# A planned decoder kernel: TensorE's operations count as ready half a microsecond behind their operands, and the index heads' rotation tables are made first

## The chip, the cores and the metric

The kernel runs on one core of one Trainium2 chip. Of the core, five engines matter: TensorE (PE in the profile, with its weight loads as PEld), VectorE (DVE), ScalarE (ACT), GpSimd (POOL) and the queue that issues most of the DMAs (SP). The metric is the device time of one execution in microseconds (us), as the median of some runs. Lower is better.

## The reference

Two layers of a decoder trunk for one sequence of 256 tokens with 1024 channels, in float32. Each layer adds three things to the residual x: a token mixer, a cross-attention into 256 memory tokens, and a SwiGLU feed-forward network of width 2816.

```python
for i in range(2):
    h = rms_norm(x, norm_mix[i])
    x = x + (dsa_moba_mixer(h, ...) if i == 0 else nsa_mixer(h, ...))
    x = x + memory_cross_attention(rms_norm(x, norm_mem[i]), rms_norm(mem, norm_mem_src[i]), ...)
    x = x + swiglu(rms_norm(x, norm_ffn[i]), ffn_w_in[i], ffn_w_out[i])

def dsa_moba_mixer(h, ...):
    aq, ak, av, iq, ik, iw, bq, bk, bv = _split(h @ w_in, AB_SIZES)
    aq, ak = partial_rope(rms_norm(aq)), partial_rope(rms_norm(ak))     # 8 heads, one key head
    iq, ik = partial_rope(iq), partial_rope(ik)                         # index heads: 8 of 32
    o_a = dsa_attention(aq, ak, av, iq, ik, iw)                         # each query keeps 64 keys
    bq, bk = partial_rope(rms_norm(bq)), partial_rope(rms_norm(bk))
    o_b = moba_attention(bq, bk, bv)                                    # 8 heads, block-sparse
    return concat(o_a, o_b) @ w_out

def nsa_mixer(h, ...):                     # 16 heads in 4 groups: compressed, selected and window branch
    q, kc, vc, ks, vs, kw, vw, gt = _split(h @ w_in, C_SIZES)
    ...
    return (g0 * o_compressed + g1 * o_selected + g2 * o_window) @ w_out
```

The rotation (partial_rope) turns the first quarter of each head by angles from the positions. So it needs tables of sine and cosine; for the heads with a norm, the kernel multiplies the norm's gain into these tables, and the index heads have no norm.

## The kernel before

The 256 tokens are two tiles of 128 (t0, t1). Every float32 product is made of three matmuls on halves (mm3): each operand is split into a high part rounded to TensorE's format and the rest, and high by high, high by low and low by high are added up. The weights stream from memory through three raw buffers (raw, 512 KB each) and are split into six buffers (whl): the high part is a cast on ACT or DVE (move), the low part a subtract on DVE. The thread that does this is the pusher. One such unit holds two blocks of 128 rows by up to 512 columns, and it serves 12 matmuls, six for each token tile.

What each engine does, and in which order, is fixed before the program runs, by a planner in Python. Each part of the computation is a thread (a generator) with a rank; it yields operations (Op), waits for flags (has, done) and waits for buffers. Est keeps an estimated clock for each engine and the estimated end of each write and read of each buffer. Steps.run repeats one step: for each engine it takes, among the operations whose estimated start lies within 0.03 us of that engine's earliest, the one of lowest rank; of these it issues the one that starts first, on its engine, and lets that thread go on. Op.best gives the estimated start, from the engine's clock and from the operands (Est.after, Est.when). An operation with two ways (either, move, tt) goes to the engine on which it would end first, so a shift of the order also moves operations between ACT, DVE and POOL. The engines then work their lists in order and wait for each other by semaphores.

The accumulators are eight: two each of mm (matmuls with weights), sp (scores), tp (transposes) and po (attention products). Names that come up below: h are the normed tokens, place and t work buffers, x the residual, di the index heads' doubled queries on their way to a transpose, hss and mrk the sums of squares of the memory keys' heads and their inverse roots (a power on POOL), stack_T the transposes of split queries (t, with identr), keys_T and mem_k those of keys (place, with ident), kvT the index scores, bv the values of the block-sparse heads. ia and ib are the index heads' rotation tables, ra and rb those with gains.

The function tables makes all rotation tables. It computes the angles, then sine and cosine on ACT. Then it waits until both norms' halves of the first tile are done, multiplies gains (kv), spreads the gains over the partitions with one small matmul (own to growt, in a tp accumulator), copies ia and ib, makes ra and rb, and the masks cm, cmn, cmi with affine selects on POOL. Its flag "tables" is what the index heads' rotation waits for, in ev_small of mixer0 (the thread that takes the narrow columns: ak, av, iq, ik, iw). Mixer 0's other rotations come later in the program and find the tables made. In the profile all planned operations carry one line, L250, so they are told apart by their buffers.

## Time and profile before

| | before |
|---|---|
| median of three runs | 789.94 us (789.73 to 790.62) |
| the profiled execution | 790.53 us, of which the span is 788.8 us |
| PE busy | 759.2 us, 96% of the span |
| DVE busy | 536.8 us, 68% |
| ACT busy | 428.5 us, 54% |
| POOL busy | 120.8 us, 15% |

The stages follow each other: mixer 0 to about 119 us, the memory attention and feed-forward of layer 0 to about 373 us, mixer 1 from there to about 527 us with its attention from about 445 to 503 us, then memory attention and feed-forward of layer 1. A timeline row gives the start, the duration, the engine, the instruction with its buffers, how many such instructions stand in a row, and in brackets the engine's idle time before it with what ended it.

### The profile page before, as it was taken

The numbers are of one execution on the slowest core, as the hardware profiler recorded it, in microseconds if no ns is written. First come the engines' busy times: TensorE is split into PE (matmuls) and PEld (weight loads), VectorE is DVE, ScalarE is ACT, GpSimd is POOL, SyncE is SP. The second block draws the span as 40 slices with busy tenths as digits, with TensorE's granted clock in tenths as the row PEclk, the third lists the DMA queues.
The fourth block names the chain that finished last, engine by engine and source line by source line (L and its number), as shares of the span: only waits on it lengthen the run. The fifth ranks groups of instructions, "written<-read, shape, count | busy, mean of one in ns | idle before, by whom it ended". The sixth has DMA issues, their size and how long they took to land.

```text
span 788.8 us, 11748 instructions
## 1 busy us (share of the span) xinstructions
PE 759.2 (96%) x4227; PEld 627.7 (80%) x4227; DVE 536.8 (68%) x1117; ACT 428.5 (54%) x819; POOL 120.8 (15%) x163
## 2 busy tenths in 40 slices
PE   6999999999999999999999998999999999999998
PEld 5777778897888889787878777877888888889886
DVE  6899999768655554455728899868677556546542
ACT  5666895665544443343627599846556434435440
POOL 1545320110000000000016355201201000000000
PEclk9999999999999999999999999999999999999999
DMA  6734246526556544767416512035435565536651
GB/s 206 226 112 132 85 145 196 169 91 198 162 162 211 187 150 155 205 237 220 129 45 181 195 47 95 27 121 162 159 114 150 167 210 185 166 116 226 219 183 53
DMA packets 70634, 122.32 MB, mean 155 GB/s; under 512 B 8548, under 2 KB 15792, under 8 KB 70576
## 3 DMA queue, kind: packets, MB, share of 16 engines
q1 hardware_dynamic: 70544, 121.58, 49.1%
q8 instruction: 33, 0.54, 0.3%
q14 instruction: 25, 0.20, 0.1%
q0 software_dynamic: 32, 0.00, 0.0%
HBM read 120.51 MB, written 1.05 MB: 154 GB/s over the span
## 4 chain that ended last, share of the span: by engine, by line
PE 69%; DVE 13%; DMA 5%; ACT 4%; issue 3%; POOL 3%; SPq 1%; ACTq 0%; POOLq 0%; DVEq 0%
PE mm L250 54%; PE po L250 8%; PE tp L250 6%; DVE whl L250 5%; DVE place L250 5%; DMA raw<-in_ffn_w_out 3%; ACT place L250 2%; ACT whl L250 2%; PE sp L250 2%; DMA raw<-in_ffn_w_in 1%; DVE rc L250 1%; POOL rope L250 1%; POOL place L250 1%; DMA raw<-in_ab_w_in 1%; DVE x L250 1%
## 5 line engine op out<-in xcount | busy, mean ns | idle before, releaser
L250 PE MATMUL mm<-whl,h 128*128 128x512 f32 (+3 forms) x1776 | 401.2, 379 | 4.7 <-DVE whl L250 4.7
L250 DVE TENSOR_TENSOR whl<-raw,whl 128x1024 fp32r<-128x1024 f32 (+3 forms) x232 | 271.2, 1173 | 138.1 <-ACT whl L250 134.0
L250 PEld LDWEIGHTS mm<-whl,h 128*128 128x128 f32 x1776 | 311.2, 189 | 62.0 <-DVE whl L250 4.6
L250 ACT ACTIVATE whl<-raw 128x1024 fp32r<-128x1024 f32 (+3 forms) x204 | 206.2, 1013 | 161.6 <-PE mm L250 43.4
L250 PE MATMUL mm<-whl,place 128*128 128x512 f32 (+1 forms) x840 | 194.4, 374 | 2.1 <-DVE x L250 1.2
L250 PEld LDWEIGHTS mm<-whl,place 128*128 128x128 f32 x840 | 142.4, 188 | 29.6 <-DVE x L250 2.1
L250 ACT ACTIVATE place<-tp 128x512 f32<-128x512 f32 (+3 forms) x123 | 56.9, 492 | 60.7 <-PE tp L250 60.5
L250 PE MATMUL po<-whl,place 128*128 128x512 f32 x264 | 68.1, 395 | 0.0
L250 PEld LDWEIGHTS po<-whl,place 128*128 128x128 f32 x264 | 49.3, 188 | 11.3
L250 PE MATMUL tp<-ident,place 128*128 128x128 f32 x340 | 54.0, 277 | 3.6 <-DVE place L250 1.6
L250 POOL TENSOR_TENSOR rh<-vh,mhalf 128x1 f32<-128x1 f32 x12 | 10.4, 867 | 274.4 <-DVE vh L250 257.7
L250 PEld LDWEIGHTS tp<-ident,place 128*128 128x128 f32 x340 | 39.2, 141 | 15.0 <-issue 4.3
L250 ACT ACTIVATE place<-place,mx 128x128 f32<-128x128 f32 (+1 forms) x96 | 42.6, 448 | 3.9 <-DVE mx L250 3.6
L250 POOL TENSOR_TENSOR place<-place,rc 128x512 f32<-128x512 f32 (+2 forms) x31 | 27.3, 883 | 38.1 <-DVE rc L250 20.2
L250 DVE CAST whl<-raw 128x1024 fp32r<-128x1024 f32 (+2 forms) x28 | 20.1, 719 | 17.0 <-PE mm L250 13.3
L250 DVE CUSTOM_DVE_ANT_0 place<-sp,cm,rq 128x128 f32<-128x128 f32 (+1 forms) x80 | 30.2, 404 | 1.2 <-PE sp L250 1.2
L250 DVE TENSOR_TENSOR x<-mm,x 128x512 f32<-128x512 f32 x36 | 24.3, 684 | 9.6 <-PE mm L250 9.6
L250 ACT ACTIVATE place<-mm,rh 128x512 f32<-128x512 f32 (+1 forms) x26 | 17.0, 655 | 25.3 <-PE mm L250 25.3
L250 ACT ACTIVATE h<-place 128x512 fp32r<-128x512 f32 x22 | 13.8, 628 | 29.0 <-DVE place L250 28.9
L250 PE MATMUL sp<-place,place 128*128 128x256 f32 x160 | 27.2, 296 | 1.6 <-DVE mx L250 1.2
L250 DVE SCALAR_TENSOR_TENSOR place<-mm,rh,place 128x512 f32<-128x512 f32 (+1 forms) x24 | 16.9, 704 | 16.9 <-PE mm L250 16.9
L250 ACT ACTIVATE place<-mm 128x512 f32<-128x512 f32 (+2 forms) x46 | 23.8, 556 | 7.4 <-PE mm L250 7.2
(203 smaller groups left out, 607.7 us busy)
## 6 DMA issues: line engine op xcount, KB each, us to landing
raw<-in_ffn_w_in SPq DMA_DIRECT2D x80, 512.0 KB, 4.4
raw<-in_ffn_w_out SPq DMA_DIRECT2D x44, 512.0 KB, 4.4
raw<-in_ab_w_in SPq DMA_DIRECT2D x16, 512.0 KB, 3.7
raw<-in_mem_w_kv SPq DMA_DIRECT2D x16, 512.0 KB, 4.6
raw<-in_nsa_w_in SPq DMA_DIRECT2D x16, 512.0 KB, 4.0
raw<-in_ab_w_out SPq DMA_DIRECT2D x8, 512.0 KB, 3.8
raw<-in_mem_w_q SPq DMA_DIRECT2D x8, 512.0 KB, 4.1
raw<-in_mem_w_o SPq DMA_DIRECT2D x8, 512.0 KB, 4.0
```

The costliest lines, as they stand in the source:

```text
L250: return f(*a, **{q: v() if q in ("start", "stop") and callable(v) else v for q, v in k.items()})
```

## The change

Two things are changed. First, the planner's estimate of when an operation of PE could start (Op.best) counts each operand that another engine wrote, and each buffer that another engine still reads, as ready 0.5 us later than estimated. Only the choice is touched: when an operation is issued, its estimated end (Est.issue) is worked out as before. Second, tables is split. ia and ib are made right behind sine and cosine, without the gains and without the wait for the norms; a new flag, "angles", says so, and the index heads' rotation waits for this one. The rest becomes gains, a thread of its own of rank 3, with the wait for the norms and the old flag "tables", for which the rotations of ak, of the queries and of bk now wait. The thread tables has rank 2 instead of 3.

```diff
+SLACK = {"PE": 0.5}
...
     def best(self):
         if self.deps is None:
-            self.deps = [self.est.after(e, outs, ins) for e, outs, ins, _, _ in self.ways]
+            self.deps = [self.est.after(e, outs, ins, SLACK.get(e, 0.0)) for e, outs, ins, _, _ in self.ways]
...
-    def when(self, ap, tab, e="", raw=True):
+    def when(self, ap, tab, e="", raw=True, slack=0.0):
         k, lo, hi = self.span(ap)
-        return max([t + HOP.get(g + e, 0.0) * (raw or e != g) for a, b, t, g in tab.get(k, ())
+        return max([t + HOP.get(g + e, 0.0) * (raw or e != g) + slack * (e != g) for a, b, t, g in tab.get(k, ())
                     if a < hi and lo < b or raw and g == "PE" != e], default=0.0)
...
-    def after(self, e, outs, ins):
+    def after(self, e, outs, ins, slack=0.0):
         t = 0.0
         for a in ins:
-            t = max(t, self.when(a, self.wr, e))
+            t = max(t, self.when(a, self.wr, e, True, slack))
         for a in outs:
-            t = max(t, self.when(a, self.wr, e, False), self.when(a, self.rd, e, False))
+            t = max(t, self.when(a, self.wr, e, False, slack), self.when(a, self.rd, e, False, slack))
...
         yield from ready(AF.Exp)
-        yield has(("mix0", 0), 2)
         nsin = cp.tile([P, NT, HALF], F32, name="nsin")
         yield V.tensor_scalar(nsin, sin, -1.0, None, op0=OP.mult)
+        for h in range(2):
+            yield V.tensor_copy(ia[:, :, h, :], cos[:, :, ::2])
+            yield V.tensor_copy(ib[:, :, h, :], (sin if h else nsin)[:, :, ::2])
+        done("angles")
+        spawn(gains(sin, nsin, cos), 3)
+
+    def gains(sin, nsin, cos):
+        yield has(("mix0", 0), 2)
...
         gv = growt.rearrange("p j (a b) -> p j a b", a=2)
-        for h in range(2):
-            yield V.tensor_copy(ia[:, :, h, :], cos[:, :, ::2])
-            yield V.tensor_copy(ib[:, :, h, :], (sin if h else nsin)[:, :, ::2])
...
-            yield has("tables")
+            yield has("angles")
             yield from rope(c[:, 128:384].rearrange("p (h d) -> p h d", h=IH), IH, ia[:, t], ib[:, t], IHALF)
...
             yield V.tensor_scalar(k, k, rk, 8.0, op0=OP.mult, op1=OP.mult)
+            yield has("tables")
             yield from rope(k, 1, ra[:, t, 1], rb[:, t, 1], HALF)
...
+                yield has("tables")
                 yield from rope(q, 8, ra[:, t, 2 * j], rb[:, t, 2 * j], HALF)
...
+            yield has("tables")
             yield from rope(q, 8, ra[:, t, 3], rb[:, t, 3], HALF)
...
-    spawn(tables(), 3)
+    spawn(tables(), 2)
```

Both changes act on the order of all engines. Three places show how.

DVE in mixer 0, around the low parts of bv's weight units (whl, numbered by buffer). Before; the last row but five is bv's second unit, the last row the third unit:

```order
L250 TENSOR_TENSOR whl_701<-raw_521,whl_701 128x1024
L250 SCALAR_TENSOR_TENSOR kvT<-place_847,iw,kvT 128x256
L250 SCALAR_TENSOR_TENSOR place_774<-tp_850,kv,place_772 128x2x128
L250 SCALAR_TENSOR_TENSOR place_775<-tp_850,kv,place_773 128x2x128
L250 SCALAR_TENSOR_TENSOR kvT<-place_847,iw,kvT 128x256
L250 MATCH_REPLACE kvT<-m_834,kvT 128x128
L250 TENSOR_TENSOR whl_862<-raw_632,whl_862 128x1024
L250 MAX m_897<-kvT 128x8
L250 TENSOR_REDUCE hss<-place_889 128x8
L250 MATCH_REPLACE kvT<-m_897,kvT 128x128
L250 TENSOR_TENSOR t_884<-place_790,t_884 128x8x64
L250 TENSOR_TENSOR whl_904<-raw_699,whl_904 128x1024
```

Now; the first row is the first unit, the last but two the second:

```order
L252 TENSOR_TENSOR whl_702<-raw_594,whl_702 128x1024
L252 MAX m_728<-kvT 128x8
L252 TENSOR_REDUCE hss<-place_718 128x8
L252 SCALAR_TENSOR_TENSOR kvT<-place_723,iw,kvT 128x256
L252 TENSOR_TENSOR t_742<-place_621,rk_631 128x1024
L252 SCALAR_TENSOR_TENSOR kvT<-place_723,iw,kvT 128x256
L252 MATCH_REPLACE kvT<-m_728,kvT 128x128
L252 TENSOR_SCALAR he<-vh_294 128x1
L252 TENSOR_TENSOR whl_733<-raw_673,whl_733 128x1024
L252 SCALAR_TENSOR_TENSOR kvT<-place_767,iw,kvT 128x256
L252 SCALAR_TENSOR_TENSOR place_755<-tp_757,kv,place_753 128x2x128
```

The second unit's subtract stands in row 128 of the list instead of 153; the third's stands in row 158 in both (the last row of before's excerpt; now it is 30 rows further than the second's).

PE in the attention of layer 1, in the second half of its heads of t0 (sp scores, tp transposes, po products). Before:

```order
L250 MATMUL sp_5140<-place_4113,place_4946 128x256
L250 MATMUL sp_5140<-place_4109,place_4946 128x256
L250 MATMUL sp_5140<-place_4113,place_4946 128x256
L250 MATMUL tp_5114<-ident,place_4963 128x128
L250 MATMUL tp_5160<-ident,place_5021 128x128 x4
L250 MATMUL po_4641<-place_5115,vv 64x128 x4
L250 MATMUL po_4641<-place_5083,vv 64x128 x4
L250 MATMUL tp_5191<-ident,place_5052 120x128
L250 MATMUL tp_5206<-identr,t_5181 128x128 x4
L250 MATMUL tp_5223<-identr,t_5181 128x128 x4
```

Now, between transposes of the same heads:

```order
L252 MATMUL tp_5118<-ident,place_4993 128x128 x2
L252 MATMUL mm_5168<-whl_4467,place_4936 128x512 x2
L252 MATMUL mm_5168<-whl_4467,place_4937 128x512
L252 MATMUL mm_5168<-whl_4467,place_4936 128x512
L252 MATMUL tp_5184<-ident,place_5008 128x128 x4
L252 MATMUL mm_5168<-whl_4467,place_4936 128x512
L252 MATMUL po_4689<-place_5119,vv 64x128 x4
L252 MATMUL po_4689<-place_5094,vv 64x128 x4
L252 MATMUL tp_5203<-ident,place_5074 128x128 x4
L252 MATMUL mm_5168<-whl_4467,place_4937 128x512
L252 MATMUL tp_5237<-ident,place_5106 120x128
L252 MATMUL mm_5168<-whl_4485,place_4936 128x512 x2
```

Matmuls of the out projection (mm, from whl and place), which before began some 60 matmuls later, stand between transposes and products now.

PE at the memory keys of layer 1 (the product with weights into mm, then the transposes of the first key tile). Before:

```order
L250 MATMUL mm_5869<-whl_5750,h_113 128x512 x2
L250 MATMUL mm_5869<-whl_5750,h_114 128x512
L250 MATMUL tp_5872<-ident,place_5810 128x128 x4
L250 MATMUL mm_5869<-whl_5750,h_113 128x512 x2
L250 MATMUL mm_5869<-whl_5750,h_114 128x512
```

Now:

```order
L252 MATMUL mm_5869<-whl_5749,h_113 128x512 x2
L252 MATMUL mm_5869<-whl_5749,h_114 128x512
L252 MATMUL mm_5869<-whl_5749,h_113 128x512 x2
L252 MATMUL tp_5872<-ident,place_5814 128x128 x4
L252 MATMUL mm_5869<-whl_5749,h_114 128x512
L252 MATMUL mm_5869<-whl_5776,h_113 128x512 x2
```

The transposes come behind five matmuls instead of three. Those of the second key tile moved from behind 18 further matmuls to behind 20. DVE at the same place, before:

```order
L250 TENSOR_TENSOR whl_5858<-raw_5794,whl_5858 128x1024
L250 TENSOR_REDUCE hss<-place_5877 128x4
L250 SCALAR_TENSOR_TENSOR mkT_5760<-tp_5872,kv,mkT_5759 128x4x128
L250 TENSOR_SCALAR he<-vm_1291 128x1
L250 TENSOR_SCALAR hss<-hss,he 128x4
L250 TENSOR_TENSOR whl_5881<-raw_5845,whl_5881 128x1024
L250 TENSOR_TENSOR place_5870<-place_5870,mrk 128x512
```

Now:

```order
L252 TENSOR_TENSOR whl_5858<-raw_5785,whl_5858 128x1024
L252 TENSOR_REDUCE hss<-place_5877 128x4
L252 TENSOR_SCALAR he<-vm_1243 128x1
L252 CAST whl_5881<-raw_5845 128x1024
L252 SCALAR_TENSOR_TENSOR mkT_5755<-tp_5872,kv,mkT_5754 128x4x128
L252 TENSOR_SCALAR hss<-hss,he 128x4
L252 TENSOR_TENSOR whl_5881<-raw_5845,whl_5881 128x1024
L252 TENSOR_TENSOR place_5870<-place_5870,mrk 128x512
```

The cast of a weight unit (CAST), which was an operation of ACT, stands between the first tile's work and hss of the second.

## Rows read from the trace of the kernel before

**Rows 1.** The page, its first part: busy time, share of the span and instructions of each engine

```profile
PE 759.2 (96%) x4227; PEld 627.7 (80%) x4227; DVE 536.8 (68%) x1117; ACT 428.5 (54%) x819; POOL 120.8 (15%) x163
```

**Rows 2.** Windows of the span: length, busy time of each engine, granted clock, DMA share, GB/s

```profile
0.00:14.65 14.65, 7.38 (x24) 5.96 (x25) 7.32 (x25) 6.48 (x11) 2.44 (x11) 1.00 0.68 206
28.00:107.00 79.00, 74.19 (x430) 58.93 (x430) 76.91 (x258) 61.20 (x144) 39.63 (x58) 0.98 0.44 131
72.70:76.10 3.40, 3.39 (x14) 2.77 (x14) 3.40 (x11) 2.37 (x6) 1.08 (x1) 0.50 0.64 190
200.00:220.00 20.00, 20.00 (x93) 16.38 (x92) 12.02 (x15) 8.16 (x12) 0.00 (x0) 1.00 0.62 189
429.00:503.00 74.00, 68.74 (x552) 58.06 (x552) 67.62 (x247) 58.75 (x183) 32.12 (x39) 1.00 0.32 108
450.00:491.00 41.00, 37.98 (x338) 32.21 (x336) 39.72 (x174) 35.54 (x124) 24.95 (x30) 1.00 0.26 87
```

**Rows 3.** Waits of PE: who waits for whom, us in total, times, longest us

```profile
PE mm L250 <- DVE whl L250: 4.9, 5, 1.9
...
PE tp L250 <- DVE place L250: 2.8, 4, 1.2
```

**Rows 4.** Timeline of PE, 26 to 41 us: start, us, instruction, count, idle before it

```profile
27.55 0.45 PE L250 MATMUL tp<-place,one 76*128 76x112 f32 x2 [1.24 <-DVE place L250]
...
27.76 7.34 PE L250 MATMUL mm<-whl,h 128*128 128x512 f32 x31
...
40.08 0.30 PE L250 MATMUL tp<-ident,di 128*128 128x128 f32 x1 [0.61 <-DVE di L250]
```

**Rows 5.** Timeline of PE, DVE and weight loads, 71 to 77 us

```profile
71.23 1.73 PE L250 MATMUL mm<-whl,h 128*128 128x512 f32 x6 [1.77 <-DVE whl L250]
...
75.25 1.22 DVE L250 TENSOR_TENSOR whl<-raw,whl 128x1024 fp32r<-128x1024 f32 x1
...
76.52 1.46 PEld L250 LDWEIGHTS mm<-whl,h 128*128 128x128 f32 x7 [0.34 <-DVE whl L250]
```

**Rows 6.** Timeline of POOL, 30 to 35 us

```profile
30.37 1.15 POOL L250 TENSOR_SCALAR_AFFINE_SELECT cm<-cm 128x128 f32<-128x128 f32 x1 [3.91 <-DVE cm L250]
...
32.46 0.32 POOL L250 TENSOR_TENSOR rope<-place,ia 128x64 f32<-128x64 f32 x1
...
33.02 1.22 POOL L250 TENSOR_TENSOR rope<-place,ib 128x32 f32<-128x32 f32 x1
```

**Rows 7.** Timeline of PE at 373 us

```profile
373.30 0.66 PE L250 MATMUL tp<-ident,x 128*128 128x128 f32 x4 [1.19 <-DVE x L250]
```

**Rows 8.** Timeline of PE, 429 to 504 us, five of the waits

```profile
429.15 0.66 PE L250 MATMUL tp<-ident,place 128*128 128x128 f32 x4 [0.76 <-POOL place L250]
...
436.38 1.87 PE L250 MATMUL mm<-whl,h 128*128 128x512 f32 x7 [0.84 <-DVE whl L250]
...
448.13 0.53 PE L250 MATMUL tp<-identr,t 128*128 128x128 f32 x4 [0.72 <-DVE t L250]
...
491.53 0.53 PE L250 MATMUL tp<-identr,t 128*128 128x128 f32 x4 [0.69 <-ACT place L250]
...
503.38 0.52 PE L250 MATMUL tp<-ident,place 128*128 128x128 f32 x3 [0.22 <-DVE place L250]
```

**Rows 9.** Timeline, 543 to 555 us: DVE, PE and POOL at the memory keys of layer 1

```profile
543.70 0.69 DVE L250 CAST whl<-raw 128x1024 fp32r<-128x1024 f32 x1 [0.19 <-PE mm L250]
...
549.19 0.63 PE L250 MATMUL tp<-ident,place 128*128 128x128 f32 x4 [0.67 <-DVE place L250]
...
551.84 1.92 POOL L250 TENSOR_TENSOR mrk<-hss,mhalf 128x4 f32<-128x4 f32 x1 [3.52 <-DVE hss L250]
...
554.63 0.63 PE L250 MATMUL tp<-ident,place 128*128 128x128 f32 x4 [0.67 <-DVE place L250]
```

**Rows 10.** Timeline of PE in the memory attention of layer 0

```profile
160.52 0.74 PE L250 MATMUL mm<-whl,place 128*128 128x256 f32 x4 [0.31 <-ACT place L250]
...
186.50 0.66 PE L250 MATMUL tp<-ident,x 128*128 128x128 f32 x4 [0.22 <-DVE x L250]
```

## The prediction

> **What bounds the kernel now.** The profiled execution took 790.53 us: a span of 788.8 us and 1.7 us around it. It stands 0.6 us above the median of the three runs, 789.94, so the sum below starts from 790.53 and is read with that half microsecond in mind. About 0.2% (1.6 us) is what a measurement of this kernel can tell from no change.
>
> I read the busy times first [rows 1]: TensorE (PE) works 759.2 us of the span, VectorE (DVE) 536.8. So PE is the bound, and what a new order can give back is PE's waiting, some 30 us, of which the first 14.65 us of the program hold a quarter (7.38 us busy) [rows 2]. Then I read the windows [rows 2]: in the feed-forward stages PE is busy 20.00 us of 20, with DVE at 12, and an order can change nothing there. It has room in the two mixers alone, and there DVE is nearly full as well: from 28 to 107 us (mixer 0) DVE works 76.91 us of 79, from 450 to 491 us (attention of layer 1) 39.72 of 41. So in these two stretches PE waits because DVE is late, and DVE has 2.1 and 1.3 us of idle time to give, no more. That is the ceiling for anything that only rearranges work there. The waits [rows 3] say the same: the largest item is weights that DVE has yet to split (whl, 4.9 us in 5 waits), then transposes whose operand DVE writes.
>
> **What the change does to an order.** A matmul in a row of matmuls takes 7.34 / 31 = 0.237 us [rows 4]. If a PE operation counts as ready half a microsecond behind its operand, the planner puts about two more independent matmuls (0.47 us) ahead of it wherever it has some. A wait shorter than that goes; a longer one becomes 0.47 us shorter; where no other matmul is at hand, nothing changes. The cost is that whoever needs the result gets it up to 0.47 us later.
>
> **1. Mixer 0: -0.3 us.** The tables' small matmul waits 1.24 us at 27.55, and the index heads' second transpose 0.61 us at 40.08, the larger of two [rows 4]. The index tables need only sine and cosine, so making them first removes the wait for the gains' matmul from the index heads' path, and the small matmul now stands ahead of aq's matmuls. If PE were free to run on, 2 us would be won. It is not. At 71.23 PE waits 1.77 us for the split of bv's second weight unit [rows 5], and whatever is won earlier only makes it arrive there earlier. The order shows the unit's subtract 25 rows further ahead on DVE, so that wait goes; but the next unit's subtract stands in row 158 of DVE in both kernels, and PE reaches its first matmul four matmuls sooner. The wait moves on by one unit. What is left is DVE's idle time: bound below -2.1 us (all of 79 - 76.91), bound above +2 (below, POOL). The rotations of the index heads run on POOL, where pieces of 0.3 us beside an idle DVE took 1.22 us beside a weight split, and the mask's affine select of 1.15 us now stands between the two tiles' rotations [rows 6]; one piece held up and this select are 0.9 + 1.15 = 2 us, in the case that the transposes, which the order puts some 20 to 30 matmuls sooner, arrive before them. I take -0.3, near the lower third, since DVE's sum of work is unchanged and its idle time is nearly nothing.
>
> The clock belongs here. Behind the 1.77 us wait the granted clock was 0.50 (1.2 of 2.4 GHz) from 72.7 to 76.1 us [rows 2], 3.4 us in which PE did 1.7 us of full-speed work; behind the 1.24 us wait at 27.55 it stayed at full. The sum gives this no price: DVE's split of the next weight unit ends at 75.25 + 1.22 = 76.47, and the weights of its first matmul are loaded at 76.52 [rows 5]. At full speed PE would have come there earlier and waited for the same split. The Trainium skill, "TensorE: Matmul & The Clock Gate", section "What's actually happening", has the throttled state as the default, which activity releases; with the wait split into small ones full speed would then be kept. By that alone this term would be -2.0 rather than -0.3; the trace agrees with the drop, and shows no time that it cost at the end.
>
> **2. Norm ahead of mixer 1: -0.5 us.** At 373.30 the transposes of x wait 1.19 us for the residual [rows 7]. They stand two matmuls later now. -0.47.
>
> **3. Mixer 1, 429 to 503 us: -2.7 us.** Eleven waits of 0.22 to 0.84 us, 5.95 us in all, of which the first, the last and the three on which the sum leans are shown [rows 8]. At 448.13 (0.72) the stacked queries' transposes come three matmuls later: -0.7. At 491.53 (0.69) and 503.38 (0.22), and at four more between 454 and 488 us (0.45, 0.44, 0.45, 0.29), they come two to six later: gone, -2.5. At 436.38 (0.84, weights) DVE has somewhat less ahead of the split: I take half, -0.4. At 429.15 the transposes now stand twelve matmuls of the narrow kind earlier, while their operand's last step goes from POOL to DVE: between -0.8 and +1.7, taken as 0. One at 483.93 gets 0.2 shorter, one at 490.34 (0.32) longer by 0.4, since the out projection's matmuls, which the order now spreads between the attention's transposes, take fillers from elsewhere. Sum -3.4. Of it 1.4 us lie between 450 and 491 us, where DVE has 1.3 us idle [rows 2]; I count half. -2.7, bounds -4.5 (74 - 68.74 = 5.3 us in which PE isn't busy [rows 2], less the 0.8 of 429.15) and 0.
>
> **4. Memory keys of layer 1: -0.3 us.** PE waits 0.67 us for each of two key tiles, at 549.19 and 554.63 [rows 9]. The first transposes come two matmuls later: -0.47. The second come four later in all, which by itself would clear the wait. But the order on DVE has a step more ahead of the second tile: the cast of a weight unit, which ACT did, is on DVE, in front of the scaling of hss; a cast took 0.69 us. The chain of hss, power on POOL (1.92 us beside a split), product (as long as the cast) then ends 0.69 later, at 555.3 instead of 554.63, by which time PE has four matmuls (0.95) more behind it than before: 0.67 - 0.95 = -0.3 for both together. Bounds -1.3 (cast covered) and +0.7 (nothing hidden).
>
> **5. Small places: +0.4 us.** In the memory attention of layer 0 a wait of 0.31 goes at 160.52; at 186.50 the norm's transposes come one matmul earlier, +0.2 [rows 10]; the same pair recurs in layer 1. Against these stand three accumulations that come two matmuls earlier in places without a wait now, up to +0.47 each. I take half of those: -0.6 + 0.4 + 0.7 = +0.5, less 0.1 for a transposes' wait in the last stage. Bounds -0.6 and +1.3.
>
> **Sum.** -0.3 - 0.5 - 2.7 - 0.3 + 0.4 = -3.4 us, so 787.1 against the profiled 790.53, and 786.5 against the median. I give 786.8.
>
> **Rivals.**
> A, swallowed. DVE sets the pace of both mixers, and PE's waits change place without getting fewer. For it: DVE's 1.3 and 2.1 us of idle time [rows 2], and a largest wait for DVE's own splits [rows 3]. Against: before 450 and behind 491 us DVE has 5 us idle. Terms 1 and 3 fall away: -0.4, so 790.1.
>
> B, slower. The attention of layer 1 is a chain: scores, maximum on DVE, exponent on ACT, transposes on PE, evacuation, product. PE's transposes are now delayed on purpose by 0.47 us each, and their results feed the engines that are the bound. There are 44 groups of transposes in that attention. If 10 of them hold DVE up, it loses 4.7 us, less the 1.3 us it has idle: +3.4, with terms 2, 4 and 5 +3.0, so 793.5. It decides from the point where DVE's idle time between 450 and 491 us grows by more than PE's waits shrink. Against it: two score tiles and two transposed tiles are in flight, so DVE mostly has other work queued.
>
> C, larger. The wait at bv's units goes entirely and DVE uses its 2.1 us; mixer 1 gives 4.0; the cast of term 4 is covered (-1.3): -2.1 - 0.5 - 4.0 - 1.3 + 0.4 = -7.5, so 783.0. It needs the 1.77 us wait not to come back at the next unit.
>
> D, the change doesn't do what it says: half a microsecond changes which matmul stands where, but the waits are longer than the fillers at hand, as at 528 us, where the position of the transposes is unchanged. 790.5.
>
> **How the numbers follow.** The forecast (784.5 to 788.8) has 0.42, A 0.21, B 0.18, C 0.12, D 0.07. Faster by over 0.2%: nine tenths of the forecast's case, C, and little of A: 0.52. Within 0.2%: the rest of the forecast's case, most of A and D, and the smallest form of B: 0.28. Slower: the rest of B and a tail of A: 0.20. The range reaches from below C's 783.0, with a little for the gross waits of term 3, to 792.5, which leaves half of B out.
>
> **What would show it.** Right: no PE wait over 0.3 us at the stacked queries' transposes; DVE between the same stages as full as now; at bv's third unit a wait of about 2 us with the clock at 0.50 behind it; the first key tile's wait at 0.2 us. Wrong: DVE's busy share in the attention of layer 1 falling below 0.95 with the stage no shorter (B); no wait over 1 us in mixer 0 (C); PE's idle time in mixer 1 still above 5 us (A).

## The result and the profile after

The changed kernel takes 785.95 us (median of 4 runs, 783.94 to 786.5) against 789.84 us before (789.68 to 790.62): a ratio of 0.9938, with a 95% interval of 0.992 to 0.9957. It is 0.6% faster, 3.9 us. In the experiments below two executions, of 930.21 and 4201.76 us, lie far outside all others and are left out of the times. The profiled execution took 785.43 us (span 783.7), 5.1 us less than the one of before.

The page's busy times of the changed kernel, as in [rows 1]:

```profile
PE 755.6 (96%) x4227; PEld 627.5 (80%) x4227; DVE 531.3 (68%) x1110; ACT 435.6 (56%) x819; POOL 123.7 (16%) x170
```

PE is still the bound. Its busy time doesn't tell what was won: it fell by 3.6 us, to 755.6, for the same 4227 matmuls, and its idle time by 1.5, from 29.6 to 28.1. Of the 3.6 us, up to 1.7 are the stretch at half clock in mixer 0 [rows 2], which the changed kernel's execution doesn't have. Also, a matmul's row lasts longer than the time to the next one's start (at 91.58 us of before, one of 128x512 lasts 0.40 us, and the next matmul starts 0.24 us after it), so the page counts the first part of a wait as work. The waits of PE by who waits for whom (us in total, times, longest), as in [rows 3]:

```profile
PE mm L252 <- DVE whl L252: 3.5, 5, 1.3
...
PE tp L252 <- DVE place L252: 3.1, 7, 0.8
...
PE tp L252 <- DVE rc L252: 2.6, 1, 2.6
...
PE tp L252 <- DVE x L252: 0.9, 2, 0.6
```

Waits for weight splits fell from 4.9 to 3.5 us, for x to 0.9. There is a new one: 2.6 us, once, for rc (the scaled softmax of mixer 0). So the gain is a difference of gains and a loss, and the first question is where each lies.

To place them, PE's own work is taken out: for each kind of PE instruction the median time from its start to the next start, added up along PE's list, is work (733 us in all). The time at which a given amount of work is done, less that amount, is what PE has lost up to there. The table gives the loss of each stage; its limits are amounts of work, which PE of before reached at 130, 410, 446 and 503 us. The first column has the start of the program in it, where one execution differs from another by up to 1 us.

| kernel | mixer 0 | layer 0's rest | front of mixer 1 | its attention | the rest | all |
|---|---|---|---|---|---|---|
| before | 26.0 | 6.0 | 2.7 | 9.9 | 6.8 | 51.4 |
| changed | 28.3 | 4.7 | 1.5 | 7.6 | 4.2 | 46.2 |

Mixer 0 lost 2.3 us; every stage behind it won, 7.4 us in all. The windows that answer to three of [rows 2] (length, busy time of each engine, granted clock, DMA share, GB/s):

```profile
28.00:107.00 79.00, 69.54 (x413) 55.03 (x411) 75.60 (x237) 58.62 (x139) 37.24 (x57) 1.00 0.46 140
429.00:503.00 74.00, 70.42 (x563) 60.38 (x562) 66.11 (x242) 63.90 (x187) 37.72 (x50) 1.00 0.39 115
450.00:491.00 41.00, 38.84 (x348) 33.59 (x346) 37.77 (x168) 37.74 (x126) 24.59 (x33) 1.00 0.30 91
```

In mixer 0 (28 to 107 us) PE is busy 69.54 us instead of 74.19 (up to 1.7 us of the difference are the stretch at half clock), and DVE 75.60 instead of 76.91: DVE, which was thought to have no idle time to lose, idles 3.4 us instead of 2.1. From 429 to 503 us PE is busy 70.42 us instead of 68.74, at a DVE that does less.

PE's waits in mixer 0, to be read beside [rows 4] and [rows 5]:

```profile
29.71 0.30 PE L252 MATMUL tp<-ident,di 128*128 128x128 f32 x1 [0.40 <-DVE di L252]
...
32.00 0.33 PE L252 MATMUL tp<-ident,di 128*128 128x128 f32 x1 [0.60 <-DVE di L252]
...
43.85 0.30 PE L252 MATMUL tp<-ident,dk 128*128 128x128 f32 x1 [1.63 <-DVE dk L252]
...
72.45 1.67 PE L252 MATMUL mm<-whl,h 128*128 128x512 f32 x6 [0.91 <-DVE whl L252]
...
75.78 3.71 PE L252 MATMUL mm<-whl,h 128*128 128x512 f32 x15 [0.54 <-DVE whl L252]
```

The index heads' transposes stand at 29.71 and 32.00 instead of 35.50 and 40.08, and wait as long as before (0.40 and 0.60). ak's transposes (dk) now wait 1.63, at 43.85. At bv's units the one wait of 1.77 us, for the second, became two, 0.91 us for the third and 0.54 for the fourth. By the measure of the table, PE of the changed kernel is 1.5 us ahead of before at 30 us, 1.9 behind at 45 us, past the wait at ak's transposes, and 0.7 ahead at 92 us. Then comes the new wait; DVE and PE there:

```profile
92.23 1.21 DVE L252 TENSOR_TENSOR whl<-raw,whl 128x1024 fp32r<-128x1024 f32 x1
...
93.36 0.68 DVE L252 TENSOR_TENSOR place<-place,rc 128x512 f32<-128x512 f32 x1
...
94.19 0.63 PE L252 MATMUL tp<-ident,place 128*128 128x128 f32 x4 [2.64 <-DVE rc L252]
```

PE's transposes wait 2.64 us for the scaled softmax tile. DVE had its sums ready at 92.16 (rc), but first split a weight unit (92.23 to 93.44), which PE doesn't need yet (in the run below that holds this split back, the first seven matmuls of the out projection, which start at 95.61 here, run before it), and then scaled the tile. In the kernel before, POOL scaled this tile, at 93.05, and the split of that unit came at 95.51.

PE's waits at the norm ahead of mixer 1 and in mixer 1, beside [rows 7] and [rows 8]:

```profile
375.04 0.66 PE L252 MATMUL tp<-ident,x 128*128 128x128 f32 x4 [0.30 <-DVE x L252]
...
432.67 1.44 PE L252 MATMUL mm<-whl,h 128*128 128x512 f32 x5 [0.39 <-DVE gt L252]
...
448.86 0.50 PE L252 MATMUL tp<-identr,t 128*128 128x128 f32 x4 [1.03 <-DVE t L252]
...
466.80 0.45 PE L252 MATMUL tp<-identr,t 128*128 128x128 f32 x3 [0.56 <-ACT place L252]
...
472.19 1.11 PE L252 MATMUL tp<-ident,place 128*128 128x128 f32 x8 [0.45 <-ACT place L252]
...
477.15 1.09 PE L252 MATMUL po<-place,vv 128*64 128x128 f32 x16 [0.87 <-ACT place L252]
...
484.95 0.53 PE L252 MATMUL tp<-identr,t 128*128 128x128 f32 x4 [0.21 <-ACT place L252]
```

The norm's wait fell from 1.19 to 0.30. From 429 to 504 us there are six waits of 0.21 to 1.03, 3.5 us in all, where eleven had 5.95. But they aren't the old ones made shorter: the stacked queries' wait at 448 grew from 0.72 to 1.03, and those at 472 and 477 us are new. The memory keys of layer 1, beside [rows 9]:

```profile
545.64 0.63 PE L252 MATMUL tp<-ident,place 128*128 128x128 f32 x4 [0.22 <-DVE place L252]
...
547.20 0.68 DVE L252 CAST whl<-raw 128x1024 fp32r<-128x1024 f32 x1
...
548.76 1.92 POOL L252 TENSOR_TENSOR mrk<-hss,mhalf 128x4 f32<-128x4 f32 x1 [4.00 <-DVE hss L252]
...
551.56 0.63 PE L252 MATMUL tp<-ident,place 128*128 128x128 f32 x4 [0.68 <-DVE place L252]
```

### The profile page after: what moved, and what is told of

Its sections match the earlier page's. It is cut to its first block, busy times and chain, and to the rows that moved or that the text cites. A ratio compares the mean times of both kernels' runs of the same rounds, so it can differ in the third digit from the quotient of the medians.

```text
span 783.7 us, 11768 instructions
## 1 busy us (share of the span) xinstructions
PE 755.6 (96%) x4227; PEld 627.5 (80%) x4227; DVE 531.3 (68%) x1110; ACT 435.6 (56%) x819; POOL 123.7 (16%) x170
## 4 chain that ended last, share of the span: by engine, by line
PE 67%; DVE 15%; DMA 9%; ACT 5%; issue 2%; POOL 1%; SPq 1%; ACTq 0%; DVEq 0%; POOLq 0%
PE mm L252 51%; PE po L252 8%; DVE whl L252 6%; PE tp L252 5%; DVE place L252 4%; DMA raw<-in_ffn_w_out 4%; ACT whl L252 3%; PE sp L252 2%; ACT place L252 2%; DMA raw<-in_nsa_w_in 2%; DMA raw<-in_ab_w_in 1%; DMA raw<-in_ffn_w_in 1%; DVE hss L252 1%; POOL rope L252 1%; DVE rc L252 1%
## 5 line engine op out<-in xcount | busy, mean ns | idle before, releaser
L252 ACT ACTIVATE whl<-raw 128x1024 fp32r<-128x1024 f32 (+3 forms) x216 | 218.6, 1013 | 193.4 <-PE mm L252 72.2
L252 PEld LDWEIGHTS mm<-whl,place 128*128 128x128 f32 x840 | 142.3, 188 | 28.8 <-DVE x L252 1.6
L252 ACT ACTIVATE place<-tp 128x512 f32<-128x512 f32 (+4 forms) x115 | 54.4, 497 | 20.9 <-PE tp L252 20.6
L252 PE MATMUL tp<-ident,place 128*128 128x128 f32 (+1 forms) x340 | 52.6, 275 | 5.8 <-DVE rc L252 2.6
L252 PEld LDWEIGHTS tp<-ident,place 128*128 128x128 f32 (+1 forms) x340 | 39.8, 140 | 15.5 <-issue 6.1
L252 POOL TENSOR_TENSOR h<-place,h 128x512 fp32r<-128x512 f32 x2 | 2.6, 1292 | 187.3 <-ACT h L252 187.3
L252 PE MATMUL sp<-place,place 128*128 128x256 f32 x160 | 26.1, 293 | 0.4 <-DVE mx L252 0.4
```

Source lines behind the costliest of these rows:

```text
L252: return f(*a, **{q: v() if q in ("start", "stop") and callable(v) else v for q, v in k.items()})
```

## The experiments

Theory T at the outset: the slack itself loses in mixer 0, where DVE is full, and wins behind it; the split of the tables matters little. Rival R: the early tables spoil mixer 0. Rival N: each order lands where it lands.

**The slack alone**: Op.best, when and after as in the change, the tables as before.

```diff
+SLACK = {"PE": 0.5}
...
-            self.deps = [self.est.after(e, outs, ins) for e, outs, ins, _, _ in self.ways]
+            self.deps = [self.est.after(e, outs, ins, SLACK.get(e, 0.0)) for e, outs, ins, _, _ in self.ways]
...
     spawn(tables(), 3)
```

> The slack of 0.5 us alone; the tables are made as before, in one thread of rank 3. In the changed kernel PE lost 2 us against before up to the end of mixer 0 (about 125 us) and won 7 us behind it. Theory T: the slack itself makes the order that loses in mixer 0, where DVE is full, and the order that wins behind it. Then this run loses about 2 us in mixer 0 too and wins about 7 behind it: 785 to 786.5. Rival R: the early tables spoil mixer 0. Then mixer 0 is as before, within 0.7 us, and the run takes about 783. Rival N: each order lands where it lands, and nothing carries over from one order to the next: behind mixer 0 the gain differs from 7 us by more than 3.

785.41 us (783.05 to 786.28), ratio 0.9932 (0.9913 to 0.9952). Mixer 0 lost 28.8 us, 2.9 more than before; behind it 7.6 us were won. R falls as the only cause: the slack alone loses in mixer 0. N's mark, a gain behind mixer 0 that differs from 7 by over 3, is not met. The trace shows where mixer 0 lost it: at 84 us PE is 0.3 us ahead of before, and between 86 and 91 us it waits 1.06 and 1.29 us for softmax products on POOL and 0.47 for ACT. The product of the longest wait took 1.45 us beside a weight split on DVE; the three before it took 0.61, 0.61 and 0.71:

```profile
87.75 1.22 DVE L251 TENSOR_TENSOR whl<-raw,whl 128x1024 fp32r<-128x1024 f32 x1
...
87.99 1.45 POOL L251 TENSOR_TENSOR place<-place,rc 128x256 f32<-128x256 f32 x1 [0.86 <-ACT place L251]
...
89.49 0.69 PE L251 MATMUL tp<-ident,place 128*128 128x128 f32 x2 [1.29 <-POOL place L251]
```

**The tables alone**:

```diff
-SLACK = {"PE": 0.5}
+SLACK = {"PE": 0.0}
```

> The index heads' tables first, without slack. Theory T: only mixer 0 is touched, and DVE is full there: within 1 us of before at the end of mixer 0, nothing behind it, 789 to 790.5. Rival R: mixer 0 loses about 2 us: 792. Rival N: behind mixer 0, where nothing was changed on purpose, the time moves by 2 us or more either way, since the order there shifts as well.

793.82 us (793.06 to 795.28), ratio 1.0046 (1.0029 to 1.0063): slower. The profiled execution lost 2.3 us in mixer 0 and 0.2 us behind it. So T's half on the tables falls too: made early, without slack, they cost as much in mixer 0 as the slack does. Three of the PE rows between 55 and 90 us, where it waits six times for DVE's splits, 0.65 to 1.21 us each:

```profile
58.62 1.66 PE L252 MATMUL mm<-whl,h 128*128 128x512 f32 x6 [1.21 <-DVE whl L252]
...
63.51 3.73 PE L252 MATMUL mm<-whl,h 128*128 128x512 f32 x15 [0.92 <-DVE whl L252]
...
80.65 0.97 PE L252 MATMUL mm<-whl,h 128*128 128x512 f32 x3 [0.99 <-DVE whl L252]
```

Before, that stretch had one wait for a split, of 1.77 us. Here PE came to each of six units before DVE had split it.

**The slack from the memory attention on, and the slack up to there**, both with early tables:

```diff
-SLACK = {"PE": 0.5}
+SLACK = {"PE": 0.0}
...
             yield from (mixer0 if L == 0 else mixer1)()
             ver += 2
...
+            SLACK["PE"] = 0.5
             yield from project(L)
```

> Both changes, but the slack is 0 until the planner reaches the memory attention of layer 0, and 0.5 us from there. Theory T: mixer 0 as in the run with the split alone (within 1 us of before), and the gain of 7 us behind it is kept: 783. Rival R: 785 to 786, as the changed kernel, with the 2 us lost in mixer 0. Rival N: a gain behind mixer 0 of less than 4 or more than 10 us.

784.72 us (783.72 to 786.6), ratio 0.993 (0.991 to 0.9949). T's 783 is missed and R's 785 to 786 is nearly met. Mixer 0 lost 2.4 us more than before, as with the tables alone, and behind it 9.2 us were won.

For the other one SLACK starts at 0.5 and is set to 0.0 at the same place.

> Both changes, but the slack is taken back to 0 from the memory attention of layer 0. Theory T: mixer 0 as in the changed kernel (2 us lost by its end, with the wait of over 2 us for a softmax product near 94 us), and nothing won behind it: about 792. Rival R says the same of mixer 0. Rival N: behind mixer 0 the time differs from before by over 2 us.

794.29 us (792.86 to 796.83), ratio 1.0054 (1.0034 to 1.0073). Its profiled execution (796.83 us) lost 4.6 us in mixer 0 and 1.7 behind it, of which a wait of 2.08 us for x at 379.77 is the largest. In mixer 0 its order is that of the changed kernel up to 94 us, and so is the wait there, of 2.63 us. With these four: three orders with slack behind mixer 0 win 7.4, 7.6 and 9.2 us there, two without it lose 0.2 and 1.7. That part is the slack's. In mixer 0 the changed kernel and these four all lose, 2.3 to 4.6 us, by whichever edit.

**The old tables and the slack from the memory attention on**, to see whether the two parts add up; the edit is made in the kernel with the slack alone:

```diff
-SLACK = {"PE": 0.5}
+SLACK = {"PE": 0.0}
...
+            SLACK["PE"] = 0.5
             yield from project(L)
```

The planner's main thread comes to this line while mixer 0's attention still runs; the orders are those of before for the first 222 rows of PE, about 90 us.

> Tables as before, slack 0 until the planner reaches the memory attention of layer 0 (the orders are those of before up to about 90 us), 0.5 us from there. Three orders with slack behind mixer 0 have won 7.4, 7.6 and 9.2 us there against before, two without it nothing; every order but that of before has lost 2.3 to 4.6 us in mixer 0. Theory T2: mixer 0 is a matter of one order among many, and that of before is a good one; the slack's gain lies behind it and adds to any of them. Then mixer 0 ends within 1.5 us of before and the run takes 781 to 784. Rival N2: the gain behind mixer 0 depends on how mixer 0 ended (it gives back what was lost there); then this run wins 5 us or less in all, 785 or more.

782.47 us (780.62 to 784.99), ratio 0.9895 (0.9876 to 0.9913). Mixer 0 lost 26.1 us, as before (26.0), and the stages behind it won 7.8. T2 holds: the gain behind mixer 0 came with each of the starts tried, and without the loss in mixer 0 the kernel is 8 us faster than before.

Its profile answers the question of the clock as well. Its order up to 90 us is that of before, with the same wait of 1.77 us at bv's second unit, but its clock didn't fall (PEclk, the number behind POOL's, is 1.00, where [rows 2] had 0.50):

```profile
73.10:76.50 3.40, 2.73 (x15) 1.78 (x14) 3.40 (x11) 2.57 (x6) 1.06 (x1) 1.00 0.58 193
```

PE in that execution, and then two rows of before:

```profile
71.65 1.67 PE L251 MATMUL mm<-whl,h 128*128 128x512 f32 x6 [1.77 <-DVE whl L251]
...
74.44 1.67 PE L251 MATMUL mm<-whl,h 128*128 128x512 f32 x6 [0.20 <-DVE whl L251]
...
76.95 2.12 PE L251 MATMUL mm<-whl,h 128*128 128x512 f32 x8 [0.84 <-DVE whl L251]
...
78.90 1.10 PE L251 MATMUL sp<-place,place 128*128 128x256 f32 x8
```

```profile
74.02 4.63 PE L250 MATMUL mm<-whl,h 128*128 128x512 f32 x14
...
78.48 1.12 PE L250 MATMUL sp<-place,place 128*128 128x256 f32 x8
```

At full clock PE waits for DVE again, 0.20 and 0.84 us; at half clock it doesn't. From the end of the wait for bv to the first scores (sp) it is 78.90 - 71.65 = 7.25 us at full clock and 78.48 - 71.23 = 7.25 us with the slow stretch. Six profiled executions share this order: those of before and of this run, and four of runs described below (slack of 0.25, slack of 1.0, and the two with a smaller slack in one attention). In four of them the clock fell to 0.50 for 3.4 us here, in two it didn't, and this time is 7.24 or 7.25 us in all six. The drop cost nothing.

**The dose**: the same kernel with 0.25 and with 1.0 in place of 0.5.

> As the run with old tables and late slack, with 0.25 us of slack. Theory: a wait goes when about as much other work is put ahead of it, and PE's waits behind mixer 0 are mostly 0.3 to 0.9 us; so half the slack wins about half, 3 to 5 us: 785 to 787. Rival: any slack that puts one matmul more ahead of each transpose is enough: 782 to 784, as with 0.5.

786.79 us (785.35 to 789.36), ratio 0.9953 (0.9936 to 0.9971): half the gain, as expected, but not made of waits that are half gone: by the table below it wins more than 0.5 us does in the attention of layer 1 and loses 2.0 us in the rest of layer 0.

> As the run with old tables and late slack, with 1.0 us of slack. Theory: the waits over 0.5 us shrink further, but the results of the transposes reach DVE and ACT up to 0.5 us later, and in the attention of layer 1 these are full; about the same as with 0.5, 781 to 785. Rival B of the prediction: the delays starve the attention of layer 1, and it gets longer by 2 us or more than with 0.5: 785 or more.

782.87 us (781.66 to 783.19), ratio 0.9898 (0.9883 to 0.9912): as with 0.5. But the stages went opposite ways:

| kernel | mixer 0 | layer 0's rest | front of mixer 1 | its attention | the rest |
|---|---|---|---|---|---|
| slack 0 (before) | 26.0 | 6.0 | 2.7 | 9.9 | 6.8 |
| slack 0 (tables alone) | 28.3 | 7.1 | 2.8 | 9.7 | 6.0 |
| 0.25 | 27.6 | 8.0 | 1.2 | 5.0 | 5.7 |
| 0.5 | 26.1 | 5.6 | 1.5 | 6.9 | 3.7 |
| 1.0 | 26.5 | 4.0 | 1.6 | 9.2 | 2.5 |

Each row is one execution. In the rest of layer 0 and behind the attention of layer 1, 1.0 is best, and 0.25 loses 2.0 or wins 1.1 us on before; in the attention, 0.25 is best and 1.0 gives nearly all back. Two PE rows of the run with 1.0, and its window from 446 to 503 us:

```profile
465.81 0.66 PE L251 MATMUL tp<-ident,place 128*128 128x128 f32 x4 [1.24 <-ACT place L251]
...
467.95 1.40 PE L251 MATMUL po<-place,vv 128*64 128x128 f32 x16 [1.13 <-ACT place L251]
```

```profile
446.00:503.00 57.00, 53.49 (x458) 46.48 (x458) 48.45 (x212) 45.24 (x154) 27.29 (x38) 0.97 0.23 71
```

PE waits 1.24 and 1.13 us for what ACT evacuates or scales, and DVE is busy 48.45 us of the 57 instead of 53.46 before, ACT 45.24 instead of 48.67: the engines that set the pace have less to do there while PE's transposes come later. That is what rival B of the prediction describes, at twice the slack. How much of the 2.3 us against 0.5 it explains is not shown: the clock of 0.97 is a stretch at half clock from 468.6 to 472.0 us, behind these two waits, in which PE is busy throughout and does 1.7 us of full-speed work in 3.4.

**Small slack in that attention, larger elsewhere**, from these rows:

```diff
+        SLACK["PE"] = 0.25
         yield from both((1, "q0"), h, KD, ev_q(0))
...
                 hi, lo, f1, f2 = oT[t, half]
+                if half and t:
+                    SLACK["PE"] = 1.0
...
+            SLACK["PE"] = 0.25 if L else 1.0
             yield from project(L)
```

> Old tables, no slack until the memory attention of layer 0, then 1.0 us, but 0.25 us in the attention of layer 1. From 446 to 503 us PE lost 9.9 us without slack, 5.0 with 0.25, 7.2 with 0.5 and 9.2 with 1.0 in the runs so far; outside of it 1.0 was best. Theory B': in that attention DVE and ACT are full, and a larger slack delays what they wait for, so the small slack is right there and the gains add: 778 to 780.5. Rival N3: the attention's time is the luck of each order, and nothing is won: 782 to 784.

780.4 us (779.27 to 781.28), ratio 0.9872 (0.9855 to 0.989). The attention lost 6.7 us instead of 9.2, not 5.0: a part of what 0.25 had won there hung on the order before.

With 0.5 in place of 1.0:

> The same with 0.5 instead of 1.0 us outside of the attention of layer 1. Theory B': 2 us better than with 0.5 throughout (782.5): 779.5 to 781.5. Rival N3: 782 to 784.

779.89 us (779.06 to 781.03), ratio 0.9872 (0.9853 to 0.989), the best of all: 10 us less than before. Its attention lost 5.05 us, as with 0.25 throughout:

```profile
446.00:503.00 57.00, 56.16 (x509) 49.01 (x509) 54.10 (x236) 50.51 (x171) 26.28 (x36) 1.00 0.21 70
```

PE is busy 56.16 of 57 us, DVE 54.10: neither is idle for long.

**DVE's order at 92 us**, in the changed kernel:

```diff
+            if i == 21:
+                yield has("sc", 5)
             yield V.tensor_tensor(u.lo, raw[:, :, :n], u.hi.bitcast(F32), op=OP.subtract)
...
         yield scale(sn, rc, n, nk)
+        done("sc")
```

> The changed kernel with one wait more in the planner: the subtract of the one weight unit that stood at 92 us on DVE, ahead of the softmax product that PE's transposes at 94.19 us wait for, may not be issued before that product. Up to there the orders are the same. Theory M: DVE's order at this one place is what mixer 0 lost its 2 us with; the wait of 2.6 us shrinks to 1.5 or less, and the run wins 1 to 2.5 us on the changed kernel: 783.5 to 785. Rival O: DVE has the same work ahead in any order, the wait turns up at another place, and the run is within 0.8 us of the changed kernel (785.95).

784.05 us (783.59 to 785.18), ratio 0.9918 (0.9903 to 0.9933): 1.9 us faster than the changed kernel by the medians, though the two intervals overlap. The same place, PE and POOL:

```profile
92.11 1.55 PE L252 MATMUL sp<-place,place 128*128 128x256 f32 x8
...
93.09 1.04 POOL L252 TENSOR_TENSOR place<-place,rc 128x512 f32<-128x512 f32 x1 [3.15 <-DVE rc L252]
...
94.19 0.66 PE L252 MATMUL tp<-ident,place 128*128 128x128 f32 x4 [0.53 <-POOL place L252]
```

The product went to POOL, as in the kernel before; PE has eight score matmuls to do ahead of the transposes, which wait 0.53 us instead of 2.64. M holds by its mark. By the measure of the table, from 90 us to the end of mixer 0 this run loses 0.7 us on before, the changed kernel 2.2, and the next run, which has the changed kernel's order there, 1.8. So one weight split in front of one product cost 1.1 to 1.5 us of what mixer 0 lost there, and not all of it.

**The cast between the key tiles**, in the changed kernel, given to ACT:

```diff
+    ON = (155,)
...
-            yield move(u.hi, raw[:, :, :n])
+            yield (S.activation(u.hi, raw[:, :, :n], AF.Copy) if i in ON else move(u.hi, raw[:, :, :n]))
```

> The changed kernel, with the cast of the one weight unit that stood on DVE (0.68 us at 547.20) between the two memory key tiles of layer 1 given to ACT, which idles 3.68 us there. Term 4 of the prediction: this cast is why the second tile's transposes still wait 0.68 us, although four more matmuls stand ahead of them. Then that wait falls to 0.1 us or less, and the stage from the first tile's transposes to the end of the memory keys is 0.5 to 0.7 us shorter. Rival: the tile waits for the power on POOL (1.92 us beside a split), which begins when the split before it ends whatever the cast does; then the wait stays above 0.4 us.

One execution, 783.47 us, so only its rows are read. The second tile's wait of 0.68 us is gone:

```profile
546.05 1.05 ACT L252 ACTIVATE whl<-raw 128x1024 fp32r<-128x1024 f32 x1
...
546.79 1.01 POOL L252 TENSOR_TENSOR mrk<-hss,mhalf 128x4 f32<-128x4 f32 x1 [2.86 <-DVE hss L252]
...
549.63 0.60 PE L252 MATMUL tp<-ident,place 128*128 128x128 f32 x4
```

From the first tile's transposes to the second's it is 549.63 - 544.80 = 4.83 us instead of 5.92, with one matmul less between (19 instead of 20), so 0.85 us were won, not 0.5 to 0.7. The rest is POOL's: the power took 1.01 us instead of 1.92, since hss was ready ahead of the next split and the power began ahead of it (546.79, split at 547.28).

**Operands alone**: in the kernel with old tables and late slack, the slack is left out for the buffers that a PE operation writes into.

```diff
-            t = max(t, self.when(a, self.wr, e, False, slack), self.when(a, self.rd, e, False, slack))
+            t = max(t, self.when(a, self.wr, e, False), self.when(a, self.rd, e, False))
```

> As the run with old tables and late slack (782.5), with the 0.5 us counted only for what a PE operation reads, and not for the accumulator that it writes into. Theory: PE's waits behind mixer 0 were nearly all for operands (transposes of what DVE, ACT or POOL write), so most of the gain is kept: 782 to 784.5. Rival: freeing of accumulators is estimated too early as well, and half the gain is lost: 785 to 787.

782.77 us (780.75 to 783.45), ratio 0.9899 (0.988 to 0.9917): the same as with both. No rows are read from this run; by its time, the gain is that of operands.

## Why the prediction was right, and where it was not

The forecast was -3.4 us, 786.8, and the median moved by -3.9 to 785.95; the profiled execution, from which the sum started, moved by -5.1. By its terms it was less good than that. Term 1 came out 2.6 us worse and term 5 some 3 us better than forecast, both outside their bounds, and term 3 a little better. That the sum landed so near is luck in part. Of its four signs of being right, one was seen, the first key tile's wait of 0.2 us.

**What the change does to an order** was right in its main line: with slack behind mixer 0 every order won 5.5 us or more there, without it none did, and it is the operands that count. The rule for single waits, that one shorter than half a microsecond goes and a longer one gets 0.47 shorter, is not what happened. Behind mixer 0 (from 128 us) before had twelve waits under half a microsecond, 3.86 us in all, and ten longer ones, 7.96 us. The changed kernel has ten, 2.99 us, and five, 3.84 us, many at other places. So it is mostly the long waits that went.

**Term 1, mixer 0: -0.3 forecast, +2.3 measured.** Two steps held: the wait at bv moved on by one unit, and the clock drop had no price, which a full-clock execution of the same order then showed. What was won early was indeed of no use, but not for the reason given: it was gone by 45 us, with the wait of 1.63 us at ak's transposes, long before bv. The step that failed was to take DVE's idle time as all that could change: "DVE's sum of work is unchanged and its idle time is nearly nothing". An engine that is nearly full can still idle more (3.4 us instead of 2.1), and what PE waits for depends on which of DVE's operations comes first. The place that cost 2.6 us, a weight split in front of a product that PE needed, was not among those that the prediction looked at. Its upper bound, +2, was about the size, but was got from POOL's rotations, where nothing happened (and the 0.3 us piece there ran beside short DVE operations, not beside an idle DVE). The rows given as its test were half wrong too: at bv's third unit there was a wait, but of 0.91 us and not 2, and the clock behind it stayed at 1.00. And neither half of the change is to blame by itself: the slack alone loses 2.9 us there, the tables alone 2.3, both 2.3. The traces name the place in all five kernels that differ from before from the start: 94 us in the changed kernel and the one with early slack, 86 to 91 us with the slack alone, and 55 to 66 us with the tables alone and with late slack, where three waits for splits, of 0.65 to 1.21 us, follow each other. Only the place at 94 us was tried by an experiment. Why those orders come to such a place, and that of before to none but its wait of 1.77 us, stays open.

**Term 2, the norm: -0.5 forecast.** The wait went from 1.19 to 0.30, -0.9. The two matmuls are not what decides it: the kernel with old tables and late slack also has its transposes two matmuls later, and waits 1.27 us there. In all three kernels a weight split that waits 0.67 to 0.98 us for its cast on ACT stands in front of the residual on DVE.

**Term 3, mixer 1: -2.7 forecast, -3.5 measured** (the two columns of the table, 12.6 to 9.1). The size was within its bounds, but its list of waits was not what happened: the one at 448 got longer, others came up. The cap from DVE's idle time between 450 and 491 us was no cap: DVE was busy 37.77 of 41 us there instead of 39.72, since some of its work had moved to ACT (37.74 of 41 instead of 35.54).

**Term 4, the memory keys: -0.3 forecast, -0.4 measured**, by its own steps: the first wait from 0.67 to 0.22, the second still 0.68 in spite of four more matmuls. The cast was the reason, as the run with the cast on ACT showed.

**Term 5, small places: +0.4 forecast.** Behind the memory keys and in layer 0 PE won about 2.5 us more than the terms above explain, outside the term's bounds of -0.6 and +1.3. The largest single part is the wait that rival D quoted, 0.93 us at 528, of transposes whose position didn't change. It is gone. Before:

```profile
526.53 1.23 DVE L250 TENSOR_TENSOR whl<-raw,whl 128x1024 fp32r<-128x1024 f32 x1 [1.54 <-ACT whl L250]
...
527.67 0.68 DVE L250 TENSOR_TENSOR x<-mm,x 128x512 f32<-128x512 f32 x1
...
528.41 0.66 PE L250 MATMUL tp<-ident,x 128*128 128x128 f32 x4 [0.93 <-DVE x L250]
```

Changed:

```profile
521.77 1.22 DVE L252 TENSOR_TENSOR whl<-raw,whl 128x1024 fp32r<-128x1024 f32 x1
...
523.30 0.68 DVE L252 TENSOR_TENSOR x<-mm,x 128x512 f32<-128x512 f32 x1
...
524.93 0.60 PE L252 MATMUL tp<-ident,x 128*128 128x128 f32 x4
```

A weight split stands in front of this residual in both. Before, the split itself waited 1.54 us for its cast on ACT, and the residual behind it came too late for PE; in the changed kernel the cast is there, and the residual is done before PE comes to it. The wait is gone in both runs without slack behind mixer 0 as well, where the stage won about 1 us, so this one isn't the slack's.

**The rivals.** A is out: mixer 1 did get shorter. B was not seen at 0.5 us; at 1.0 us the attention of layer 1 was longer than at 0.5, as B has it. C's size (783.0) was reached by the kernel without the loss in mixer 0 (782.47), not by its mechanism. D is out: the same tables with and without 0.5 us of slack behind mixer 0 differ by 8 to 9 us in three pairs (785.95 and 794.29, 784.72 and 793.82, 782.47 and 790.52).

## What to carry to other kernels

Where a planner's estimate makes a bound engine wait a little at many places, counting its operands as ready later than estimated puts filler there, and the right amount differs by stage: set it where the other engines have room, and keep it small where they are full, since each result comes later. Read the list of the second engine for long operations that aren't urgent (here weight splits of 1.2 us, some of which wait themselves) in front of short ones that the bound engine needs; its busy share doesn't show them. When two edits of an order are bundled, time them by stage: here one stage's loss hid a third of the gain.

## What the runs showed of the hardware

The same wait of 1.77 us at the same place of the same order was followed by a granted clock of 0.50 for 3.4 us in four profiled executions and of 1.00 in two others, and a longer one, 2.64 us, was not followed by a drop (the wait, then what follows; clock 1.00 in both):

```profile
91.50:94.20 2.70, 0.06 (x3) 0.04 (x1) 2.70 (x11) 2.70 (x13) 0.00 (x0) 1.00 0.04 17
94.20:98.00 3.80, 3.27 (x21) 2.73 (x22) 3.80 (x12) 3.06 (x9) 1.97 (x2) 1.00 0.60 209
```

So the length of a wait alone, as these rows have it, didn't tell whether the clock falls, and where PE stands behind another engine a fall may cost nothing (7.24 or 7.25 us to the first scores in all six). The Trainium skill's "TensorE: Matmul & The Clock Gate", section "What's actually happening", which the prediction cited, has the clock follow activity; these rows neither show more of the rule nor let one foretell a drop.

A power of 128x4 on POOL took 1.92 us when DVE had begun a subtract of two operands of 128x1024 0.17 us ahead of it, and 1.01 us when it began first; the subtract took 1.22 us both times. A wide product on POOL does hold the subtract up: at 432.53 us in the changed kernel it took 2.08 us, having begun when a product of 128x512 on POOL had 1.0 us left. The Trainium skill, "SBUF — State Buffer", section "Who interferes with whom", has a DVE instruction with two inputs in SBUF contend with a GpSimd instruction that reads it, and lets the order of issue decide which of them is blocked. The traces agree for the power behind the split and for the split behind the product. The split behind the small power was not held up, and there the measurement stands.
